# Attention probabilities turned in 32x32 blocks by VectorE, value products on row tiles of 32, heads in two groups

## The chip, the cores and the metric

The kernel runs on one core of one Trainium2 chip. The metric is the device time of one execution in microseconds (us), as the median of several runs. All inputs start in the chip's main memory and all outputs end there.

## The reference

One step of a decoder layer over two inputs at once: a prompt of 512 tokens, and one new token for each of eight running sequences ("samples"). The width is 1024, and everything is float32. Cut to what matters here:

```python
h = einsum('btd,de->bte', x, w_in)                  # 1024 -> 3600 columns
qa, ka, va, za, ga, qb, kb, vb, gb = split(h)       # mixer A: 4 heads; mixer B: 8 heads of 64
o_a, s_new = gla_chunked(...)                       # mixer A: gated linear attention, chunks of 64
# mixer B, prompt: every query reads earlier keys at three strides
for window, dil in ((128, 1), (512, 4), (2048, 16)):
    p = exp(logits + bias - m)                      # logits = q.k / 8
    outs.append(einsum('bhqj,bqjhd->bhqd', p, vg) / s)
o_b = merge of the three, weighted by their sums
mix = concat([o_a * silu(ga), o_b * silu(gb)])
y   = einsum('bte,ed->btd', mix, w_out)
x_new = layer_norm(alpha * x + y)
# outputs: x_new, the GLA states, and the new key and value rows
```

For the prompt the three strided patterns make one causal attention over 512 keys, in which a key's weight carries how many of the patterns reach it. So mixer B is, for each head: scores (512 x 512, the lower triangle in blocks of 128), an exponential with a bias table, a normalization by the row's sum, and the product of the probabilities with the values.

## The kernel before, in words

**Engines and order.** No order of instructions is written down. Each part of the work is a Python generator that yields operations and conditions; `add(gen, rank)` hands it to a planner (class `Plan`), which issues, at each step, the operation that its cost model lets start first, and among equals the one of the lowest rank. `T`, `V`, `S`, `G` and `D` are TensorE (PE in the profile), VectorE (DVE), ScalarE (ACT), GpSimd (POOL) and SyncE's DMA queue (SP). A `Batch` is issued without anything between; `At(name, n)` waits until a mark was set n times. When two operations stand as a pair, the planner takes the engine that is done first: so `copy` goes to VectorE or ScalarE. Constants of the model (`LATE`, `SWITCH`, `SPARE` and transfer rates) shift what it chooses, not what an operation does. All instructions are issued from one line of code, L366 before and L368 after, so the profile tells them apart by tile names.

**Buffers.** `SLOTS` gives the number of buffers of each kind in SBUF (raw weights `r`, split weights `w`, 4 KB tiles `g`, probabilities `pr`, turned probabilities `pt`, bias strips `st` and so on), and `BANKS` the eight PSUM banks: three for projections (`d`), three for scores (`s`), two more (`t`).

**Projections.** PE's main work. Each weight and each input is split into a high and a low part (`hi_`, `lo_`), and three products are summed for each of eight blocks of 128 inputs. `feature` makes columns on partitions (two halves of 256 tokens, the first with the eight samples beside it); `token` makes tokens on partitions. The order is ka, qa, qb, kb, vb, gb, va, ga, and then the output projection (`ps_y`, `ps_yf`). Weights come group by group over SP's queue (`weight_loads`, tiles `raw`).

**Mixer B of the prompt, the part that changes.** `strips` builds the bias strip of each head and query half, two buffers' worth ahead. `scores(m, pi, qt)` makes, for head pair m and query half pi, the score blocks of two query blocks in one batch of PE (tile `ps_s`). `softmax(h, q, ...)` then does, for one head and one query block of 128: a multiply with the strip and a row maximum on VectorE (shown as CUSTOM_DVE_ANT_0, `pr<-ps_s,strip`), an exponential on ScalarE, a reciprocal and a scale. The probabilities lie with queries on partitions; the product with the values needs keys there. So each 128x128 block goes through PE's transpose into `ps_pt`, and `copy` brings it to `pt`, one tile for each head and query half:

```python
for k in range(q + 1):
    yield T.transpose(pt[:, k * P:k * P + P], pr[:, k * P:k * P + P], ident)
yield copy(B[f"pt{h}{pi}"][:, :q + 1, qs], pt[:, :n]...)
```

There are 80 such blocks. `weighted(g, pi)` waits for the four heads of group g in query half pi, and issues one batch: for each key block and head, 64 columns of values as the weights (128 rows of contraction) and up to 256 queries as the moving side, into one bank `ps_pv`. One `copy` brings the bank to `obT`. There are four such batches. `mix_b` multiplies `obT` by the gate `gb` and splits the product for the output projection.

**Other work at the same time.** Mixer A's chunks on PE are short runs of small products (`ps_l`, `ps_og`, `ps_kv`, `ps_oa`). The samples' attention over the cached keys and values is elementwise work of GpSimd and VectorE (`past`, `vv`). `keys_store` brings the 512 key rows of the prompt to memory, as 16 transfers at the end of the kernel; `values_store` does the same for the values.

Of the kernel before, what the change touches and what calls it, by code (L numbers as in the profile page):

```python
# [62 lines left out]
    g=24,  # L63
    w=6, r=2,
    sv=5,
    pt=4,
    t2=3, st=3,
    pr=4,
    t1=6, ob=4,
# [6 lines left out]
LATE = 1600.0  # L76
SWITCH = 105
PIECE = 256
SPARE = 800.0


class Op:
# [3 lines left out]
    def __init__(self, eng, fn, args, kw):  # L86
# [13 lines left out]
        if fn == "dma_start":  # L100
# [4 lines left out]
            rate = 60 if run <= 128 else 175 if x.ap[0][1] <= 64 else 340 if run >= 4096 else 230  # L105
# [265 lines left out]
def trunk(ctx: ExitStack, tc: tile.TileContext, xT, xp, xs, state, ck, cv, w_in, wab, gnorm,  # L371
# [140 lines left out]
    order = [g for k, g in groups.items() if k not in ("ka0", "ka1")] + wo  # L512
# [33 lines left out]
    def first_loads():  # L546
# [16 lines left out]
        add(weight_loads(), 3)  # L563
# [9 lines left out]
    def first_splits():  # L573
# [27 lines left out]
        add(weight_splits(), 4)  # L601
# [83 lines left out]
    def gates(n, own):  # L685
        for u in range(2):
            yield from make(f"{n}{u}", Need("g", f"{n}{u}", [P, 4, 256]))
        for i in range(4):
            yield from feature(groups[f"{n}{i}"], gate_into(n, own, i))

    def dense():
# [24 lines left out]
        add(gate_decay(pz), 10)  # L716
# [5 lines left out]
        for i in range(2):  # L722
            yield from feature(groups[f"qa{i}"], into("qa", qa_s, i, 0.125))
        for x in ("qh0", "ql0", "qh1", "ql1"):
            yield from make(x, Need("g", x, [P, 4, 256], F32R), 4)
        for i in range(4):
            yield from feature(groups[f"qb{i}"], parts("q", q_s, i, 0.125))
        for i in range(4):
            yield from make(f"kp{i}", Need("g", f"kp{i}", [P, 2, 512], F32R), 2)
            yield from feature(groups[f"kb{i}"], parts("k", k_s, i, 1.0))  # L730
        for u in range(2):
            yield from make(f"v{u}", Need("g", f"v{u}", [P, 2, 512]))
        for i in range(2):
            yield from token(groups[f"vb{i}"], *vb_into(i))
        yield from gates("gb", gb_s)
        for u in range(2):
            yield from make(f"va{u}", Need("g", f"va{u}", [P, 2, 512]))
        for i in range(2):
            yield from token(groups[f"va{i}"], *va_into(i))
        yield from gates("ga", ga_s)  # L740
        free(*xt)
        for t in range(TT):
            add(residual(t), 8)
# [153 lines left out]
    def gla_state():  # L897
# [3 lines left out]
        yield At("qb", 8)  # L901
# [114 lines left out]
    def parts(n, own, m, scale):  # L1016

        def evac(ps, u):
            if n == "q":
                h, l = (B[f"q{x}{u}"][:, m, :] for x in "hl")  # L1020
            else:
                h, l = (B[f"kp{m}"][:, x, u * 256:u * 256 + 256] for x in range(2))
            yield S.mul(h, ps[:, :256], scale)
            yield V.scalar_tensor_tensor(l, ps[:, :256], scale, h.bitcast(F32), op0=ALU.mult, op1=ALU.subtract)
            if u == 0:
                yield S.mul(own[:, m, :], ps[:, 256:TW[0]], scale)
            mark(f"{n}b{m}{u}")
            mark(f"{n}b")
            if n == "k":
                add(keys_out(ps, m, u), 2)  # L1030
            else:
                free(ps)
        return evac

    def keys_out(ps, m, u):
# [6 lines left out]
        mark("kw")  # L1042

    def keys_store():

        yield At("kw", 8)
        yield At("y0_done", 1)
        for i in range(2):
            kw = B[f"kw{i}"].rearrange("p m (b j) -> p m b j", j=32)
            for m in range(2):  # L1050
                for a in range(4):
                    c = (2 * i + m) * P + a * 32
                    yield D.dma_start(kw_p[:, c:c + 32].rearrange("(b i) j -> i b j", i=32), kw[a * 32:a * 32 + 32, m])
            free(B[f"kw{i}"])
# [30 lines left out]
    def vb_into(i):  # L1085
        def evac_f(ps, f):
            c = slice(i * GW + f * P, i * GW + f * P + P)
# [4 lines left out]
            yield copy(B["v0"][:, :, c], ps[:, :GW].rearrange("p (t c) -> p t c", t=2))  # L1092
            free(ps)
            mark(f"vb{i}0")

        def evac(ps, t):
            yield copy(B["v1"][:, t - 2, i * GW:i * GW + GW], ps)
            free(ps)
            mark(f"vb{i}1")
        return evac_f, evac  # L1100

    def values_store(u):
        for i in range(2):
            yield At(f"vb{i}{u}", 2)
        yield D.dma_start(vw_p[u * GW:u * GW + GW, :].rearrange("(t p) c -> p t c", p=P), B[f"v{u}"])

    def strips():
        yield At("tab")
        yield At("qb", 1)
        for pi in range(2):  # L1110
            w = 256 * (pi + 1)
            for h in range(HB):
# [9 lines left out]
    def scores(m, pi, qt):  # L1122
# [8 lines left out]
        own = pi  # L1131
        for v in range(2):
# [8 lines left out]
        kp, qx = B[f"kp{m}"], [B[f"q{x}{pi}"] for x in "hl"]  # L1141
        yield Batch(T.matmul(ps[v, q][:, cols[q]], qx[a][v * 64:v * 64 + 64, m, (q % 2) * P:(q % 2) * P + P],
# [3 lines left out]
        for v in range(2):  # L1146
# [3 lines left out]
            for q in qt:  # L1150
                add(softmax(2 * m + v, q, ps[v, q], pr[v, q], cols[q]), 31 + 20 * pi / 100 + m / 50)

    def softmax(h, q, ps_all, pr_all, cols):
# [3 lines left out]
        qs = slice(j * P, j * P + P)  # L1157
# [10 lines left out]
        if j == 0:  # L1168
            yield from make(f"pt{h}{pi}", Need("pt", f"pt{h}{pi}", [P, 2 * pi + 2, 256]))
        else:  # L1170
            yield At(f"pt{h}{pi}")
# [6 lines left out]
        mark(f"p{h}{pi}")  # L1178
        if h == HB - 1 and j == 1:
            mark("scores")  # L1180

    def weighted(g, pi):
# [5 lines left out]
        for h in hs:  # L1188
            yield At(f"p{h}{pi}", 2)
        for u in range(pi + 1):  # L1190
            yield At(f"vb{g}{u}", 2)
        yield from make(f"obT{pi}{g}", Need("ob", f"obT{pi}{g}", [P, 2, 256]), 2)
        pv = yield bank(("s", "t"), f"ps_pv{g}{pi}")
        last = 2 * pi + 1
        pts = [B[f"pt{h}{pi}"] for h in hs]
        every = [(k, h) for k in range(last + 1) for h in range(4)]
# [3 lines left out]
        free(*pts)  # L1200
        yield copy(B[f"obT{pi}{g}"].rearrange("p m t -> p (m t)"), pv)
        free(pv)
        for m in (2 * g, 2 * g + 1):
            mark(f"ob{pi}{m}")
            mark(f"ob{pi}")
        if plan.marks[f"ob{pi}"] == 4 and pi:
            free(B["v0"], B["v1"])

    def sample_queries():
# [3 lines left out]
        for bi in range(NB):  # L1213
            qbc = yield Need("t2", f"qbc{bi}", [P, 512])
            yield D.dma_start(qbc, qsd[bi:bi + 1, :].to_broadcast([P, 512]))
            past = yield Need("sv", f"past{bi}", [P, 2, 512])
            yield D.dma_start(past, ck[bi])
            add(sample_logit(bi, past, qbc), 50)

    def sample_logit(bi, past, qbc):  # L1220
        for k in range(2):
            for c in range(0, 512, PIECE):
                x = past[:, k, c:c + PIECE]
                yield G.tensor_tensor(x, x, qbc[:, c:c + PIECE], op=ALU.mult)
        yield V.tensor_reduce(lt[:, :, bi * 8:bi * 8 + 8], past.rearrange("p k (h d) -> p k h d", d=64), axis=AX.X, op=ALU.add)
        free(past, qbc)
        mark("lt")

    def sample_softmax():
# [17 lines left out]
        raw = yield Need("pr", "cts_raw", [66, T_W - T_D])  # L1247
# [47 lines left out]
    def sample_value(bi, vv, pb):  # L1295
        vf = vv.rearrange("p k f -> p (k f)")
        pf = pb.rearrange("p m k -> p (m k)")
        for c in range(0, 2 * 512, PIECE):
            x = vf[:, c:c + PIECE]
            yield G.tensor_tensor(x, x, pf[:, c:c + PIECE], op=ALU.mult)  # L1300
        yield V.tensor_reduce(o_pv[:, :, bi], vf.rearrange("p (m k) -> p m k", m=4), axis=AX.X, op=ALU.add)
        free(vv, pb)
# [93 lines left out]
    def gate_into(n, own, m):  # L1396
        def evac(ps, u):
# [7 lines left out]
            yield V.tensor_tensor(B[f"{n}{u}"][:, m, :], ps[:, :256], sg[:, :256], op=ALU.mult)  # L1405
# [8 lines left out]
    def mix_tiles(n, u):  # L1414
# [3 lines left out]
        else:  # L1418
            yield At(f"ob{u}0")
            yield At(f"gb{u}0")  # L1420
        for x in "hl":
            yield from make(f"m{x}{n}{u}", Need("g", f"m{x}{n}{u}", [P, 4, TW[u]], F32R))
# [21 lines left out]

    def mix_b(u, m):
        yield At(f"ob{u}{m}")
        yield At(f"gb{u}{m}")
        yield At(f"mlb{u}")
        gb = B[f"gb{u}"][:, m, :]
        yield V.tensor_tensor(gb, gb, B[f"obT{u}{m // 2}"][:, m % 2], op=ALU.mult)  # L1450
        free(B[f"obT{u}{m // 2}"])
        yield from split(gb, B[f"mhb{u}"][:, m, :GW], B[f"mlb{u}"][:, m, :GW])
        mark(f"mix_b{u}{m}")
        mark(f"mix_b{u}")
        if plan.marks[f"mix_b{u}"] == 4:
            free(B[f"gb{u}"])
# [10 lines left out]
    def mix_sample_b():  # L1467
        yield At("gb_s", 4)
        yield At("o_bs")
        yield At("mlb0")  # L1470
        yield V.tensor_tensor(gb_s, gb_s, o_bs, op=ALU.mult)
        yield from split(gb_s, B["mhb0"][:, :, GW:], B["mlb0"][:, :, GW:])
# [21 lines left out]
    def out_unit(t, c, w):  # L1494
# [3 lines left out]
        for k in range(KT):  # L1498
            yield g.at(k)
            yield At(f"mix_b{u}{k}") if k < 4 else At(f"mix_a{u}", t % 2 + 1)  # L1500
            mh, ml = (B[f"m{x}{'ba'[k // 4]}{u}"][:, k % 4, tl] for x in "hl")
# [15 lines left out]
    def out_half(g, f, ps, ks):  # L1517
        w, c = wo[g // 2], g % 2 * GW + f * P
        for k in ks:
# [3 lines left out]
            mh, ml = (B[f"m{x}{'ba'[k // 4]}0"][:, k % 4, :] for x in "hl")  # L1523
# [98 lines left out]
    add(fills(), 9)  # L1622
    add(dense(), 100)
    add(bias_table(), 60)
# [132 lines left out]
```

## Time and profile before

| what | value |
|---|---|
| median of 3 runs | 283.76 us (283.2 to 284.01) |
| the profiled execution's own time | 283.35 us |
| its span, first to last instruction | 281.5 us |
| granted TensorE clock, mean | 0.991 |
| busy share of the span | PE 96%, weight loads 90%, VectorE 73%, ScalarE 56%, GpSimd 20% |
| DMA | 52.27 MB, mean 186 GB/s |

The profile is one execution. PE counts matmuls and PEld the weight loads that run beside them. A busy share is a mean over stages with different limits. The groups name an operation by its output and inputs (`out<-in`), with partitions x elements and a count; behind the bars stand busy time, the mean duration of one in ns, and the idle time before it with what ended it. In the chain of waits each row is a start, a duration and the work that was on the path at that time; "issue" is time in which the engine waited for nothing that the profile shows. PE's float32 products leave two records each; those on split inputs one.

### The profile page before, as it was taken

The page shows a single profiled execution, that of the slowest core. Times are in us where ns is not written, and L with a number is a line of the kernel's source. Part 1 is how long each engine was busy: PE and PEld are TensorE (multiplying, and loading weights), DVE is VectorE, ACT ScalarE, POOL GpSimd, SP SyncE. Part 2 cuts the span into 40 slices and gives each one's busy share as a digit, 9 for nine tenths or more (in the row PEclk, how much of TensorE's full clock was granted, in tenths as well). Part 3 has the DMA queues.
Part 4 walks back from the last instruction along what each step waited for, and adds up shares of the span by engine and source line. Part 5 has one row for each costly group of instructions (what it writes and reads, how often), then busy time and mean ns, then how long its engine had stood idle before and what let it go on. Part 6 is the DMA issues. An engine that isn't in the chain of part 4 may idle for free.

```text
span 281.5 us, 7063 instructions
## 1 busy us (share of the span) xinstructions
PE 271.2 (96%) x2760; PEld 253.3 (90%) x2760; DVE 206.2 (73%) x501; ACT 158.5 (56%) x448; POOL 55.4 (20%) x72
## 2 busy tenths in 40 slices
PE   8999999999999999999999999999999999999980
PEld 5899999999989999998979989999899999997880
DVE  3856799978967956649768885537987997539575
ACT  4748754514745974668677863425589955413011
POOL 4000000000282472700003535824500000000000
PEclk9999999999999999999999999999999999999996
DMA  7966628323876798647499889599563499865203
GB/s 201 286 173 187 184 77 220 83 77 108 276 219 180 236 285 241 160 160 230 155 226 179 231 225 265 119 251 191 180 198 102 150 336 255 189 139 197 105 2 149
DMA packets 59944, 52.27 MB, mean 186 GB/s; under 512 B 12506, under 2 KB 50692, under 8 KB 59910
## 3 DMA queue, kind: packets, MB, share of 16 engines
q1 hardware_dynamic: 59802, 51.73, 67.3%
q8 instruction: 22, 0.36, 0.6%
q14 instruction: 12, 0.10, 0.1%
q10 hardware_dynamic: 108, 0.07, 0.1%
HBM read 46.24 MB, written 6.03 MB: 186 GB/s over the span
## 4 chain that ended last, share of the span: by engine, by line
PE 91%; DVE 4%; DMA 2%; ACT 1%; issue 1%; SPq 0%; DVEq 0%
PE ps_ga L366 8%; PE ps_gb L366 8%; PE ps_qb L366 8%; PE ps_yf L366 8%; PE ps_y L366 7%; PE ps_kb L366 7%; PE ps_va_f L366 4%; PE ps_qa L366 4%; PE ps_vb_f L366 4%; PE ps_va L366 4%; PE ps_vb L366 4%; PE ps_pt L366 3%; PE ps_pv L366 3%; PE ps_s L366 3%; PE ps_ka L366 3%; DMA x_raw<-in_xT_dram 2%
## 5 line engine op out<-in xcount | busy, mean ns | idle before, releaser
L366 POOL TENSOR_TENSOR past<-past,qbc 128x256 f32<-128x256 f32 x32 | 25.3, 824 | 89.0 <-DMA past<-in_ck_dram 89.0
L366 POOL TENSOR_TENSOR vv<-vv,pb 128x256 f32<-128x256 f32 x32 | 26.9, 872 | 55.7 <-DMA pb<-psd_s 47.8
L366 ACT ACTIVATE pr<-pr,ms 128x128 f32<-128x128 f32 (+3 forms) x47 | 24.8, 545 | 5.9 <-DVE ms L366 5.9
L366 DVE CUSTOM_DVE_ANT_0 pr<-ps_s,strip 128x128 f32<-128x128 f32 (+3 forms) x32 | 14.5, 479 | 2.6 <-PE ps_s L366 2.5
L366 PE MATMUL ps_pt<-cf,pr 128*128 128x128 f32 x80 | 13.6, 275 | 0.3 <-DVE pr L366 0.3
L366 PE MATMUL ps_ka<-xx,hi_ka 128*128 128x264 f32 (+1 forms) x64 | 13.4, 306 | 0.5 <-DVE xx L366 0.5
L366 ACT ACTIVATE sg<-sg 128x264 f32<-128x264 f32 (+1 forms) x32 | 13.6, 426 | 0.3
L366 ACT COPY pt<-ps_pt 128x256 f32<-128x256 f32 (+3 forms) x25 | 10.4, 431 | 5.8 <-PE ps_pt L366 5.6
L366 PEld LDWEIGHTS ps_ka<-xx,hi_ka 128*128 128x128 f32 x64 | 10.9, 203 | 1.5 <-DVE xx L366 0.9
L366 ACT ACTIVATE d<-d 128x512 f32<-128x512 f32 x11 | 6.8, 643 | 6.7 <-DVE d L366 6.7
L366 PEld LDWEIGHTS ps_pt<-cf,pr 128*128 128x128 f32 x80 | 9.3, 140 | 1.1 <-issue 1.0
L366 ACT ACTIVATE rstd<-mv 128x1 f32<-128x1 f32 x4 | 0.7, 203 | 16.8 <-DVE mv L366 16.8
L366 DVE TENSOR_REDUCE o_pv<-vv 128x4 f32<-128x1024 f32 x8 | 9.7, 1210 | 0.2 <-POOL vv L366 0.2
L366 DVE TENSOR_REDUCE lt<-past 128x16 f32<-128x1024 f32 x8 | 9.6, 1204 | 0.0
L366 PE MATMUL ps_pv<-pt,v 128*64 128x256 f32 (+1 forms) x96 | 9.5, 348 | 0.0
L366 PE MATMUL ps_ka<-xx,lo_ka 128*128 128x264 f32 (+1 forms) x32 | 9.4, 293 | 0.0
L366 PEld LDWEIGHTS ps_pv<-pt,v 128*64 128x64 f32 x96 | 6.3, 137 | 2.9
L366 DVE TENSOR_SCALAR pr<-pr,ms 128x512 f32<-128x512 f32 (+3 forms) x17 | 8.4, 498 | 0.4
L366 ACT COPY feat_y<-ps_yf 128x256 f32<-128x256 f32 x8 | 3.0, 372 | 9.9 <-PE ps_yf L366 9.9
L366 DVE TENSOR_TENSOR xx<-x_raw,xx 128x520 fp32r<-128x520 f32 (+2 forms) x9 | 5.8, 640 | 3.6 <-ACT xx L366 3.5
L366 PE MATMUL ps_s<-kp,qh 64*128 64x128 f32 (+3 forms) x64 | 8.3, 344 | 0.0
L366 DVE TENSOR_TENSOR d<-b 128x1024 f32<-128x1024 f32 x6 | 7.3, 1217 | 0.0
(529 smaller groups left out, 1028.1 us busy)
## 6 DMA issues: line engine op xcount, KB each, us to landing
past<-in_ck_dram SPq DMA_DIRECT2D x8, 512.0 KB
vv<-in_cv_dram SPq DMA_DIRECT2D x8, 512.0 KB
pb<-psd_s SPq DMA_DIRECT2D x16, 256.0 KB
s<-in_state_dram SPq DMA_DIRECT2D x4, 512.0 KB
qbc<-qsd SPq DMA_DIRECT2D x8, 256.0 KB
strip<-tabr SPq DMA_DIRECT2D x8, 256.0 KB
y<-in_xp_dram SPq DMA_DIRECT2D x4, 512.0 KB
x_raw<-in_xT_dram SPq DMA_DIRECT2D x7, 260.0 KB
```

Source lines behind the costliest of these rows:

```text
L366: getattr(eng.eng, op.fn)(*op.args, **op.kw)
```

## The change

It does five things.

1. The probabilities are turned by one VectorE instruction for each head and query block, `V.transpose`, which transposes each 32x32 block in its place and leaves the blocks where they are. PE's 80 transposes and the 32 copies from PSUM are gone. `pt` is one tile for each head now, with all four query blocks.
2. After that, the four row blocks of 32 partitions in `pt` belong to the four 32-blocks of queries in each query block; the columns go by 32-blocks of keys, and within one the 32 keys lie on the partitions and the 32 queries on the columns. So a value product contracts over 32 rows only. For row block r, key block k and rotation d, `probs` picks the columns of the key 32-block (r + d) mod 4, in all query blocks from k on. The values of those keys must lie on the same 32 partitions: `values_rotate(g)` makes three copies of each value tile, rotated by 32, 64 and 96 partitions, by DMA within SBUF (tiles `vr`, two transfers each).
3. `weighted(g)` runs once for each group of four heads, with all 512 queries: 256 products of 32 rows and 64 columns (4 key blocks x 4 rotations x 4 heads x 4 row blocks), with 128, 96, 64 or 32 moving columns, into four banks, one for each row block of queries, and four copies to `obT`.
4. Tiles `qh`, `ql`, `gb`, `mhb`, `mlb` and the value tiles are cut by head group in place of token half. The scores of the second head group wait until the first group's value batch has its banks (`At("pv0")`). The value projection vb0 comes ahead of kb2.
5. Buffers, model constants and the ranks of nearly all tasks are set anew. The key rows are stored in two parts in the middle, and no longer at the end.

The diff, cut to its core:

```diff
-    g=24,
-    w=6, r=2,
+    g=21,
+    w=7, r=3,
...
-    t2=3, st=3,
+    t2=2, st=2,
...
-    t1=6, ob=4,
+    t1=5, ob=2,
...
-LATE = 1600.0
-SWITCH = 105
+LATE = 1300.0
+SWITCH = 140
...
-SPARE = 800.0
+SPARE = 1100.0
+
+ORDER = "qa0 qa1 qb0 qb1 qb2 qb3 kb0 kb1 vb0 kb2 kb3 vb1 gb0 gb1 gb2 gb3 va0 va1 ga0 ga1 ga2 ga3".split()
...
-            rate = 60 if run <= 128 else 175 if x.ap[0][1] <= 64 else 340 if run >= 4096 else 230
+            rate = 130 if run <= 128 else 175 if x.ap[0][1] <= 64 else 340 if run >= 4096 else 230
...
-        yield At("kw", 8)
-        yield At("y0_done", 1)
...
+        yield At(f"kw_in{i}", 4)
...
+    def values_rotate(g):
...
+        yield At(f"vb{g}", 4)
+        vr = yield Pair(*(Need("g", f"vr{g}{d}", [P, TT, GW]) for d in range(1, 4)))
+        for d, r in enumerate(vr, 1):
+            B["vr", g, d] = r
+            c = P - d * 32
+            yield D.dma_start(r[:c], B[f"v{g}"][d * 32:])
+            yield D.dma_start(r[c:], B[f"v{g}"][:d * 32])
+            mark(f"vr{g}")
...
+        if m > 1:
+            yield At("pv0")
...
-        if j == 0:
-            yield from make(f"pt{h}{pi}", Need("pt", f"pt{h}{pi}", [P, 2 * pi + 2, 256]))
+        if q == 0:
+            yield from make(f"pt{h}", Need("pt", f"pt{h}", [P, 3 * 384 + NP]))
...
-        pt = yield bank("t", f"ps_pt{h}{q}")
-        for k in range(q + 1):
-            yield T.transpose(pt[:, k * P:k * P + P], pr[:, k * P:k * P + P], ident)
+        yield V.transpose(B[f"pt{h}"][:, q * 384:q * 384 + n], pr)
         free(pr_all)
-        yield copy(B[f"pt{h}{pi}"][:, :q + 1, qs], pt[:, :n].rearrange("p (k t) -> p k t", t=P))
-        free(pt)
...
         hs = range(4 * g, 4 * g + 4)
         for h in hs:
-            yield At(f"p{h}{pi}", 2)
...
+            yield At(f"p{h}", TT)
+        yield At(f"vr{g}", 3)
+        yield from make(f"obT{g}", Need("ob", f"obT{g}", [P, 2, NP]), 4)
+        pv = yield Pair(*(bank(("s", "t"), f"ps_pv{g}{r}") for r in range(4)))
+        mark(f"pv{g}")
...
-        yield Batch(T.matmul(pv[h % 2 * 64:h % 2 * 64 + 64, h // 2 * GW + (P if k == last else 0):h // 2 * GW + GW],
-                             B[f"v{k // 2}"][:, k % 2, (4 * g + h) * 64:(4 * g + h) * 64 + 64], pts[h][:, k, P if k == last else 0:],
-                             start=k == 0 and h < 2, stop=k == last, skip_group_check=True) for k, h in every)
...
+        def probs(h, r, k, d):
+            x = pts[h][r * 32:r * 32 + 32]
+            return bass.AP(tensor=x.tensor, offset=x.offset + k * 384 + k * P + (r + d) % 4 * 32, ap=[x.ap[0], [384, TT - k], [1, 32]])
+
+        yield Batch(T.matmul(pv[r][h % 2 * 64:h % 2 * 64 + 64, h // 2 * P + k * 32:h // 2 * P + P],
+                             vs[d][r * 32:r * 32 + 32, k, h * 64:h * 64 + 64], probs(h, r, k, d),
+                             start=k + d == 0 and h < 2, stop=k + d == 6, skip_group_check=True)
+                    for k in range(TT) for d in range(4) for h in range(4) for r in range(4))
+        free(*pts, *vs)
+        ob = B[f"obT{g}"].rearrange("p m (q r t) -> p m q r t", r=4, t=32)
+        for r in range(4):
+            yield copy(ob[:, :, :, r, :], pv[r][:, :2 * P].rearrange("p (m q t) -> p m q t", m=2, t=32))
+            free(pv[r])
```

More of the change, by code (lines that the diff above doesn't have):

```diff
@@ L511, in trunk @@
     wo = [Group(w_out, g * 512, f"wo{g}_", 512) for g in range(2)]
-    order = [g for k, g in groups.items() if k not in ("ka0", "ka1")] + wo
+    order = [groups[k] for k in ORDER] + wo
     def weight_loads():
@@ L683, in into, with project @@
         return evac
[L685 to L689, printed above, removed]
+    def project(n, i):
+        g = groups[f"{n}{i}"]
+        if n == "qa":
+            yield from feature(g, into("qa", qa_s, i, 0.125))
+        elif n == "qb":
+            if i % 2 == 0:
+                for x in "hl":
+                    yield from make(f"q{x}{i // 2}", Need("g", f"q{x}{i // 2}", [P, 2, NP], F32R), 4)
+            yield from feature(g, parts("q", q_s, i, 0.125))
+        elif n == "kb":
+            yield from make(f"kp{i}", Need("g", f"kp{i}", [P, 2, 512], F32R), 2)
+            yield from feature(g, parts("k", k_s, i, 1.0))
+        elif n == "vb":
+            yield from make(f"v{i}", Need("g", f"v{i}", [P, TT, GW]), 2)
+            yield from token(g, *vb_into(i))
+        elif n == "va":
+            if i == 0:
+                for u in range(2):
+                    yield from make(f"va{u}", Need("g", f"va{u}", [P, 2, 512]))
+            yield from token(g, *va_into(i))
+        elif n == "gb":
+            if i % 2 == 0:
+                yield from make(f"gb{i // 2}", Need("g", f"gb{i // 2}", [P, 2, NP]))
+            yield from feature(g, gate_into("gb", gb_s, i))
+        else:
+            if i == 0:
+                for u in range(2):
+                    yield from make(f"ga{u}", Need("g", f"ga{u}", [P, 4, 256]))
+            yield from feature(g, gate_into("ga", ga_s, i))
     def dense():
@@ L721, in dense @@
                 add(into("ka", ka_s, i, 1.0)(pk[i, u], u), 2)
[L722 to L740, printed above, removed]
+        for name in ORDER:
+            yield from project(name[:2], int(name[2]))
         free(*xt)
         for t in range(TT):
-            add(residual(t), 8)
+            add(residual(t), 46.7)
         add(residual_sample(), 8)
@@ L1109, in strips @@
         yield At("qb", 1)
-        for pi in range(2):
+        for h0, pi in ((0, 0), (0, 1), (4, 0), (4, 1)):
             w = 256 * (pi + 1)
-            for h in range(HB):
+            for h in range(h0, h0 + 4):
                 yield At(f"kb{h // 2}{pi}")
@@ L1175, in softmax, with weighted @@
         free(pr_all)
-        yield copy(B[f"pt{h}{pi}"][:, :q + 1, qs], pt[:, :n].rearrange("p (k t) -> p k t", t=P))
-        free(pt)
[L1178 to L1182, printed above, removed]
+        mark(f"p{h}")
+    def weighted(g):
         hs = range(4 * g, 4 * g + 4)
         for h in hs:
-            yield At(f"p{h}{pi}", 2)
[L1190 to L1196, printed above, removed]
-        yield Batch(T.matmul(pv[h % 2 * 64:h % 2 * 64 + 64, h // 2 * GW + (P if k == last else 0):h // 2 * GW + GW],
-                             B[f"v{k // 2}"][:, k % 2, (4 * g + h) * 64:(4 * g + h) * 64 + 64], pts[h][:, k, P if k == last else 0:],
-                             start=k == 0 and h < 2, stop=k == last, skip_group_check=True) for k, h in every)
-        free(*pts)
-        yield copy(B[f"obT{pi}{g}"].rearrange("p m t -> p (m t)"), pv)
-        free(pv)
@@ L1203, in weighted @@
         for m in (2 * g, 2 * g + 1):
[L1204 to L1207, printed above, removed]
+            for u in range(2):
+                mark(f"ob{u}{m}")
+                mark(f"ob{u}")
     def sample_queries():
@@ L1443, in mix_a, with mix_of @@
             free(ga)
+    def mix_of(n, u, k):
+        if n == "a":
+            return [B[f"m{x}a{u}"][:, k, :] for x in "hl"]
+        return [B[f"m{x}b{k // 2}"][:, k % 2, TS[u]] for x in "hl"]
     def mix_b(u, m):
+        g = m // 2
         yield At(f"ob{u}{m}")
         yield At(f"gb{u}{m}")
[L1448 to L1452, printed above, removed]
+        yield At(f"mlb{g}")
+        gb = B[f"gb{g}"][:, m % 2, u * GW:u * GW + GW]
+        yield V.tensor_tensor(gb, gb, B[f"obT{g}"][:, m % 2, u * GW:u * GW + GW], op=ALU.mult)
+        free(B[f"obT{g}"])
+        yield from split(gb, *(x[:, :GW] for x in mix_of("b", u, m)))
         mark(f"mix_b{u}{m}")
-        mark(f"mix_b{u}")
-        if plan.marks[f"mix_b{u}"] == 4:
-            free(B[f"gb{u}"])
+        mark(f"mixed{g}")
+        if plan.marks[f"mixed{g}"] == 4:
+            free(B[f"gb{g}"])
     def mix_sample_a():
@@ L1470, in mix_sample_b @@
         yield At("mlb0")
+        yield At("mlb1")
         yield V.tensor_tensor(gb_s, gb_s, o_bs, op=ALU.mult)
-        yield from split(gb_s, B["mhb0"][:, :, GW:], B["mlb0"][:, :, GW:])
+        for g in range(2):
+            yield from split(gb_s[:, 2 * g:2 * g + 2], *(B[f"m{x}b{g}"][:, :, GW:TW[0]] for x in "hl"))
         mark("mix_sb")
```

127 lines of the change are left out of this document (64 added, 63 removed).

## The prediction

> **What bounds the kernel now.** I read the page's shares first, then PE's waits, the chain of waits in order of time, the stages as windows, and the instruction queue.
>
> ```profile
> PE 271.2 (96%) x2760; PEld 253.3 (90%) x2760; DVE 206.2 (73%) x501; ACT 158.5 (56%) x448; POOL 55.4 (20%) x72
> ...
> PE 91%; DVE 4%; DMA 2%; ACT 1%; issue 1%; SPq 0%; DVEq 0%
> ...
> q8 instruction: 22, 0.36, 0.6%
> ...
> PE warm_ps L366 <- DVE warm L1617: 1.2, 1, 1.2
> PE ps_ka L366 <- DVE xx L366: 0.5, 2, 0.3
> PE ps_qb L366 <- issue: 0.5, 1, 0.5
> PE ps_pt L366 <- DVE pr L366: 0.3, 1, 0.3
> ```
>
> PE is busy for 96% of the span and makes 91% of the chain. The last four rows are everything that PE waited for. So a microsecond taken from PE comes off the time, and one added to PE or made PE wait goes onto it. The other engines count only where they make PE wait. PE's rows of the stages that the change touches, from the chain of waits (start, us, what, records):
>
> ```profile
> 46.52 2.00 PE ps_l L366 x128
> ...
> 54.48 1.01 PE ps_og L366 x32
> 55.49 2.00 PE ps_l L366 x128
> 57.49 0.44 PE ps_qb L366 x2
> 57.94 0.50 issue
> ...
> 106.27 1.45 PE ps_pv L366 x16
> ...
> 122.95 1.45 PE ps_pv L366 x16
> ...
> 142.18 3.18 PE ps_pv L366 x32
> ...
> 157.03 0.76 PE ps_pt L366 x7
> ...
> 166.01 3.18 PE ps_pv L366 x32
> ...
> 193.56 1.03 PE ps_kv L366 x32
> ...
> 212.13 2.12 PE ps_oa L366 x96
> ```
>
> **Removed: the transposes of the probabilities on PE.** Seven transposes in a row take 0.76 us, 0.109 us each.
>
> ```profile
> L366 PE MATMUL ps_pt<-cf,pr 128*128 128x128 f32 x80 | 13.6, 275 | 0.3 <-DVE pr L366 0.3
> ```
>
> The group's mean of 275 ns overlaps with its neighbours, so I take the chain's pace: 80 x 0.109 = 8.7 us off PE. The four old batches of value products cost 1.45 + 1.45 + 3.18 + 3.18 = 9.3 us and go as well.
>
> **Added: two batches of 256 value products.** Each product has 32 rows of contraction and 64 columns of weights, so eight lie on PE side by side: four row tiles by two column tiles. In the old batches every f32 product left two records (48 products, 96 records), so a batch now has 512 records, in rounds of eight, 16 rounds at each moving width of 128, 96, 64 and 32. Do eight really run at once? ps_oa's 96 records are 32 on four tiles and 64 on eight. At ps_kv's pace (four tiles, 32 records in 1.03 us) the 32 take 1.03, which leaves 1.09 us for the 64; on four tiles they would need 2.06. So yes, on two row groups by four column groups; four by two is not in the trace. Price of a round: width 256 and 128 together give the old batches' 3.18 us for 12 rounds of 256 and 4 of 128 on two tiles, so 0.227 us for 256 and 0.114 for 128. Width 96 is three quarters of that, 0.086. For 64 and 32 a floor holds: ps_l loads 64 columns for a width of 32 and needs 2.00 us for 32 rounds, 0.0625 each. A batch is 16 x (0.114 + 0.086 + 0.0625 + 0.0625) = 5.2 us, both 10.4. On work alone PE loses 8.7 and gains 1.1.
>
> **Whether the instructions come in time** decides the sign. PE has 2760 matmuls and as many weight loads, 5520 instructions, and the instruction queue brought 22 packets with 0.36 MB: one packet feeds 251 instructions. At the usual pace of a projection that lasts over 14 us:
>
> ```profile
> 22.90 10.27 PE ps_qa L366 x84
> ```
>
> (10.27 / 84 is 0.122 us for a load and a matmul.) ps_og and ps_l, back to back, are 160 records, so 320 instructions in 3.01 us; two records later PE stops for 0.50 us with nothing that the profile can name. A single ps_l, 256 instructions (at 46.52), has no such stop behind it. My reading: PE holds the packet it executes and the next one, and a run longer than that waits for a packet. From 54.48 to 58.44 it executed 324 instructions in 3.95 us: 251 in 3.1 us. A new batch has 1024 instructions, 4.1 packets, and needs one each 1.3 us. With the first at hand and three awaited, it takes 3 x 3.1 + 1.3 = 10.6 us instead of 5.2, both 21.2. The ends: the queue's share of 0.6% of 16 engines' 281.5 us is 27 us, 1.23 us a packet, which would cost nothing (10.4); a packet for each 3.95 us gives 3 x 3.95 + 1.3 = 13.2, both 26.4. I take 3.1, the only stretch in which PE ran dry.
>
> The Trainium skill, "Runtime: NRT & Kernel Launch", section Instruction fetch mechanics, says that the sequencer streams 16 KiB blocks of 256 instructions by itself while the current one executes, at a cost "mostly hidden"; by it the batches stay at 5.2 us, the first rival below. The trace agrees with the block's size and disagrees at the one row of 0.50 us.
>
> In the new order of PE's instructions ps_og no longer stands next to a ps_l (31 projection matmuls stand before ps_og and 19 behind it): the 0.50 us go.
>
> **Moved to other engines.** VectorE turns 32 blocks of 128 to 512 columns.
>
> ```profile
> L366 DVE STREAM_TRANSPOSE kw<-ps_kb 128x256 f32<-128x256 f32 x8 | 3.5, 443 | 1.1 <-ACT k_s L366 1.1
> ...
> L366 DVE CUSTOM_DVE_ANT_0 pr<-ps_s,strip 128x512 f32<-128x512 f32 x8 | 5.4, 680 | 0.1
> ...
> L366 DVE CUSTOM_DVE_ANT_0 pr<-ps_s,strip 128x128 f32<-128x128 f32 x8 | 2.2, 275 | 0.0
> ...
> L366 DVE COPY pt<-ps_pt x7: 281/558/692, 108.0 to 157.4; 128x384 f32<-128x384 f32 x3, 128x128 f32<-128x128 f32 x2, 128x256 f32<-128x256 f32 x1, 128x512 f32<-128x512 f32 x1
> ```
>
> 443 ns at 256 columns, and 0.135 us for each 128 more or less as in the other two rows ((680 - 275) / 3): 0.31, 0.44, 0.58 and 0.71, eight of each, 16.3 us. About 3.4 us of VectorE's copies of transposes go (seven, near 0.5 each). That is +12.9 us on VectorE in the stretch of the scores:
>
> ```profile
> 64.00:95.00 31.00, 30.66 (x369) 29.62 (x362) 26.26 (x66) 17.77 (x55) 12.97 (x16) 1.00 0.65 198
> 95.00:127.00 32.00, 32.00 (x279) 29.94 (x278) 20.17 (x59) 21.05 (x61) 12.35 (x16) 1.00 0.75 218
> 127.00:165.00 38.00, 38.00 (x319) 34.60 (x317) 31.33 (x86) 30.26 (x75) 9.38 (x12) 1.00 0.83 208
> ```
>
> (PE, loads, VectorE, ScalarE, GpSimd; then clock, DMA share, GB/s.) VectorE goes from 77.8 to 90.7 us. With starved batches PE's side of this stretch is 101 - 8.7 + 11.9 = 104 us, so VectorE is 87% full, as in 64 to 95 now (26.26 of 31): I cost it at nothing, and PE's own waits are what hides it. ScalarE loses 25 copies and gains eight smaller ones: nothing.
>
> Six rotated copies of the values, 0.5 MB each, join SP's queue and the DMA engines: 3 MB at some 210 GB/s are 14 us of DMA, spread over some 60 us whose share is 0.75 to 0.83. In the new order each set stands behind key stores and ahead of the va weights. The keys' 16 stores come from the end to the middle:
>
> ```profile
> 236.15 14.01 SPq L366 DMA_DIRECT2D out_dram<-kw  x16
> ```
>
> 0.88 us of SP each. What hides them is one more raw weight buffer (three for two) and one more split one (seven for six); if that cover goes, a late weight group stops PE for what is missing, 1 to 3 us. Whole heads now wait in one batch for 16 softmaxes, and behind it on PE stand the gb and va projections. From the last scores to each batch PE has 84 and 96 projection matmuls, 10 and 11.7 us, against about 9 and 10.6 us of VectorE work in its order: nothing, or 1 to 2 us if it lags. The last normalization is the same.
>
> **The sum**, against the profiled execution's own 283.35 us: - 8.7 (transposes) - 9.3 (old products) + 21.2 (new ones) - 0.5 (the old stop) = 286.1. The median of the runs is 0.4 above the profiled one: 286.4. Its own bounds, from packets every 2.5 us to every 3.95 us: 283 to 292.
>
> **Rivals.** *Packets are in time.* For it: 22 packets came and one stop of 0.50 us is all that shows; one case is thin. Against it: a stop exactly behind the longest fast run. Then 283.35 - 8.7 - 9.3 + 10.4 - 0.5 = 275.3, plus up to 3 us of VectorE's lag as PE no longer waits: 277 with the 0.4. It decides if a packet takes under 1.3 us. Faster, chance 0.25.
>
> *VectorE becomes the bound.* With packets in time the stretch of 101 us would have to shrink to 93, and VectorE's 90.7 us would fill 97% of it. No stretch above shows more than 85%; at 90% the stretch takes 101 us again and the gain is gone: 283, between 281 and 286. For it: two thirds of the added work stand in chains score, exponential, scale, turn. Against it: PE's 24 to 96 matmuls of cover. 0.12.
>
> *Records, not columns, price a product.* If ps_l's 2.00 / 128 = 0.0156 us were a floor for every record, 1024 records take 16.0 us: 280.9, 281.3 with the 0.4. Against it: ps_oa's 1.09 us for 64 records is 0.017, explained as well by width. 0.05. The Trainium skill, "TensorE: Matmul & The Clock Gate", section "Wait — 56ns, not 53.3ns?", gives a floor of about 25 ns from start to start; by it the batches take 25.6 us and the kernel 290.5. ps_l's 15.6 ns speaks against that floor here, so it gets no chance of its own.
>
> **How the numbers follow.** Forecast 0.58. A change of 0.3%, 0.85 us, is about what a measurement of this kernel can tell from none. Faster: 0.25 + 0.05 + 0.04 of VectorE + 0.03 of the forecast's low end = 0.37; within: 0.07 + 0.03 = 0.10; slower: 0.48 + 0.05 = 0.53. The range 276.8 to 290 leaves out the fastest part of the first rival (about 0.1) and packets slower than some 3.6 us (0.08). Alone, the forecast would have 283 to 290.
>
> **What would show it.** Right: two batches ps_pv near 10 us each in the chain, with stops put down to issue inside them and some 28 packets on the instruction queue (5520 - 160 - 192 + 2048 = 7216 instructions). Batches near 5 us without such stops make it the first rival; near 8 us with even pace, the third. PE waiting for VectorE's pt ahead of ps_pv, or for ps_s's banks, is the second. Rows "PE <- DMA raw" would mean that SP's queue was late. ps_pt must be gone. It is wrong if PE's idle time hardly grows.

## The result, and the profile after

The changed kernel takes 305.33 us (304.87 to 307.1, four runs), against 283.48 us for the kernel before in the same comparison: 1.077 times as long, 95% interval 1.074 to 1.081. Here and below a median is of all executions, while a ratio and its interval leave out the executions in a slower state, at a lower clock or over 1.5% above the fastest of their kernel. The profiled execution took 307.1 us with a span of 305.3. From the page of the kernel after, the busy shares, the chain and the instruction queue, and then what PE waited for most:

```profile
PE 275.6 (90%) x3608; PEld 259.3 (85%) x3608; DVE 214.3 (70%) x520; ACT 149.6 (49%) x435; POOL 54.3 (18%) x72
...
PE 74%; DVE 9%; issue 7%; ACT 6%; DMA 3%; SPq 0%; DVEq 0%
...
q8 instruction: 28, 0.46, 0.6%
...
PE ps_pv L368 <- issue: 17.8, 6, 5.2
PE warm_ps L368 <- DVE warm L1651: 1.2, 1, 1.2
PE ps_gb L368 <- DVE gb L368: 1.1, 1, 1.1
```

PE's idle time grew from 10.3 to 29.7 us (span less busy time), and nearly all of the growth is one row: six stops inside ps_pv, 17.8 us, with nothing behind them that the profile names. VectorE has a smaller share of the longer span than before (70% for 73%). The two value batches in the chain of waits (start, us, what):

```profile
123.97 3.37 PE ps_pv L368 x191
127.34 2.12 issue
129.46 1.66 PE ps_pv L368 x81
131.12 4.26 issue
135.38 1.82 PE ps_pv L368 x104
137.20 1.63 issue
138.83 0.64 PE ps_pv L368 x21
...
180.55 2.81 PE ps_pv L368 x172
183.36 5.15 issue
188.51 2.62 PE ps_pv L368 x114
191.14 3.02 issue
194.16 2.15 PE ps_pv L368 x105
196.31 1.58 issue
197.89 1.17 PE ps_pv L368 x58
199.06 3.92 PE ps_va L368 x17
```

The first batch lasts from 123.97 to 139.47, 15.5 us, the second from 180.55 to 199.06, 18.5 us. (The chain drops some records of a run; in the trace the middle runs are 128 records long, 256 instructions with their weight loads, one packet.) The last row shows a second loss: 17 projection matmuls take 3.92 us, 0.23 us each, where the prediction's row for ps_qa had 0.122. The windows around the batches say why (PE, loads, VectorE, ScalarE, GpSimd; then clock, DMA share, GB/s):

```profile
124.00:136.00 12.00, 5.62 (x425) 5.33 (x427) 3.25 (x16) 4.29 (x14) 2.87 (x4) 1.00 0.72 211
136.00:139.50 3.50, 1.87 (x113) 1.69 (x101) 0.76 (x3) 0.09 (x1) 0.00 (x0) 0.52 0.57 167
139.50:146.40 6.90, 6.90 (x36) 6.45 (x37) 1.61 (x3) 2.05 (x5) 0.00 (x0) 0.50 0.58 148
146.40:180.40 34.00, 32.42 (x262) 30.71 (x261) 30.78 (x89) 23.08 (x67) 6.58 (x8) 1.00 0.84 179
...
187.30:199.00 11.70, 5.88 (x321) 5.49 (x320) 0.00 (x0) 0.00 (x0) 5.76 (x9) 0.50 0.23 68
199.00:204.40 5.40, 5.40 (x29) 5.40 (x26) 2.14 (x5) 3.90 (x9) 0.00 (x0) 0.50 0.00 0
```

Around the stops of 4.26 and 5.15 us the granted clock falls to 0.50, and it stays there while PE works again: 6.9 us behind the first batch and 5.4 us behind the second. At half speed these 12.3 us do the work of 6.1.

So the account of the profiled execution: 283.35 - 8.7 (transposes) - 9.3 (old products) - 0.5 (the old stop) + 34.0 (both batches) + 6.1 (half clock behind them) = 305.0. Other waits of PE grew from 0.8 to 3.2 us (all its rows of waits, without the first one of 1.2 and without issue), which gives 307.4 against 307.1 measured.

### The profile page after: what moved, and what is told of

It is laid out like the page before. It is cut to its first block, busy times and chain, and to the rows that moved or that the text cites. A ratio compares the mean times of both kernels' runs of the same rounds, so it can differ in the third digit from the quotient of the medians.

```text
span 305.3 us, 8766 instructions
## 1 busy us (share of the span) xinstructions
PE 275.6 (90%) x3608; PEld 259.3 (85%) x3608; DVE 214.3 (70%) x520; ACT 149.6 (49%) x435; POOL 54.3 (18%) x72
## 4 chain that ended last, share of the span: by engine, by line
PE 74%; DVE 9%; issue 7%; ACT 6%; DMA 3%; SPq 0%; DVEq 0%
PE ps_qb L368 8%; PE ps_kb L368 8%; PE ps_yf L368 8%; PE ps_y L368 7%; PE ps_pv L368 5%; PE ps_ga L368 5%; PE ps_va L368 4%; PE ps_gb L368 4%; PE ps_qa L368 4%; PE ps_vb_f L368 4%; PE ps_va_f L368 3%; DMA raw_ka<-in_w_in_dram 3%; PE ps_s L368 3%; DVE pr L368 2%; PE ps_l L368 2%
## 5 line engine op out<-in xcount | busy, mean ns | idle before, releaser
L368 POOL TENSOR_TENSOR vv<-vv,pb 128x256 f32<-128x256 f32 x32 | 25.7, 834 | 81.3 <-DMA pb<-psd_s 81.3
L368 PE MATMUL ps_pv<-pt,vr 32*64 32x128 f32 (+3 forms) x768 | 15.0, 282 | 17.8 <-issue 17.8
L368 ACT ACTIVATE pr<-pr,ms 128x128 f32<-128x128 f32 (+3 forms) x50 | 26.2, 542 | 8.8 <-DVE ms L368 8.4
L368 PEld LDWEIGHTS ps_pv<-pt,vr 32*64 32x64 f32 x768 | 12.8, 163 | 18.7 <-issue 18.7
L368 DVE STREAM_TRANSPOSE pt<-pr 128x128 f32<-128x128 f32 (+3 forms) x32 | 15.0, 491 | 10.1 <-PE ps_pv L368 9.4
L368 ACT COPY obT<-ps_pv 128x256 f32<-128x256 f32 x8 | 2.4, 387 | 29.2 <-PE ps_pv L368 29.2
L368 DVE TENSOR_TENSOR gb<-gb,obT 128x256 f32<-128x256 f32 x8 | 3.1, 416 | 18.8 <-ACT obT L368 18.8
L368 DVE COPY_PREDICATED near<-cm,ps_l 128x256 f32<-128x256 uint8 x12 | 6.3, 545 | 3.9 <-PE ps_l L368 3.7
L368 PE MATMUL ps_gb<-xx,hi_gb__1666 128*128 128x264 f32 (+1 forms) x32 | 8.3, 360 | 0.5 <-ACT v L368 0.5
L368 ACT COPY feat_y<-ps_yf 128x256 f32<-128x256 f32 x8 | 3.0, 370 | 10.2 <-PE ps_yf L368 10.2
```

What stands on the lines that cost most here:

```text
L368: getattr(eng.eng, op.fn)(*op.args, **op.kw)
```

## Experiments

Theories, as the expectations number them. 1: PE gets packets of 256 instructions too slowly for a batch that executes one in 1.5 us. 2: the regrouping and the ranks cost the time. 3: the 32-row tiles themselves stop PE. 4, 5 and 6 come up below, for what is left when the stops are gone. In the tables, "packets" is PE's waits put down to issue, "others" its other waits without the first one of 1.2 us, both summed from the rows of PE's waits in the profiled execution.

**The stops made in the kernel before.** No part of the change is in this kernel, only more instructions in a row:

```diff
-                    for i, (_, _, ks, qs) in enumerate(made)
+                    for _ in range(4) for i, (_, _, ks, qs) in enumerate(made)
```

> The kernel before, with the products of mixer A's levels (ps_l) made four times over into the same places (same outputs): batches of 512, 512 and 256 records, 1024, 1024 and 512 instructions, on 64-row tiles, with no change elsewhere. By their own pace of 2.00 us for 128 records they add 15 us. Theory 1, a packet of 256 instructions each 3.7 us at best: the large batches take 12 to 14 us in place of 8.0, with stops put down to issue after runs of 128 records and a granted clock below 1 behind them; 283.4 + 15 + 2 x 5 + some 3 to 6 for the clock = 311 to 315 us. Theory 3, stops belong to 32-row tiles or to the rotated copies: no stops, 298.5 us.

Measured: 323.45 us (one execution), and all three batches have 512 records, not two of 512 and one of 256. Their own added work is thus 3 x 6.0 = 18 us. From its chain of waits, two of the three batches, and the window of the first of these:

```profile
68.57 4.02 PE ps_l L366 x265
72.58 0.82 issue
73.40 2.06 PE ps_l L366 x128
75.47 1.66 issue
77.13 3.15 PE ps_l L366 x119
...
88.43 3.27 PE ps_l L366 x214
91.71 1.57 issue
93.28 2.61 PE ps_l L366 x128
95.89 1.12 issue
97.01 3.64 PE ps_l L366 x128
100.73 1.49 PE ps_l L366 x42
...
62.00:82.00 20.00, 17.52 (x591) 16.70 (x584) 7.36 (x14) 4.35 (x9) 0.00 (x0) 0.84 0.01 3
```

After some 210 to 265 records comes the first stop, then runs of exactly 128 records. From the start of one such run to the start of what follows it are 3.73 us each time (73.40 to 77.13, 93.28 to 97.01, 97.01 to 100.73; in the last of these the clock is 0.50, and PE's own work fills 3.64 of it). In the window shown the DMA engines are at 1% and 3 GB/s. So neither the 32-row tiles (these are 64 rows) nor other transfers are needed for the stops: 256 instructions took 3.73 us here once PE lived from packet to packet, 14.6 ns an instruction. The clock of 0.84 shows the half clock again. Theory 1's time of 311 to 315 was for one batch less: with three large ones its sum is 283.4 + 18 + 3 x 5 + 4.5 to 9 for the clock = 321 to 325. Theory 3 fails.

**A quarter of the instructions.** The same columns pass through PE; a product takes all 128 rows:

```diff
-                             vs[d][r * 32:r * 32 + 32, k, h * 64:h * 64 + 64], probs(h, r, k, d),
+                             vs[d][:, k, h * 64:h * 64 + 64], probs(h, k, d),
...
-                    for k in range(TT) for d in range(4) for h in range(4) for r in range(4))
+                    for k in range(TT) for d in range(4) for h in range(4))
```

> The changed kernel, with each value batch made of 64 products over all 128 rows in place of 256 products over 32 (each rotation goes to one bank; what is left out is the sorting of the queries by row block, so the attention output of the prompt is another one). The columns that pass through PE in a round, VectorE's turns, the rotated copies and all waits stay; PE's instructions for a batch fall from 1024 to 256, one packet. Theory 1, PE runs out of instruction packets: no stop put down to issue in ps_pv, a batch near 5.2 us, the granted clock stays at 1.00 behind it, and the time is 305.3 - 17.8 (stops) - about 6 (batches' own work, 16 to 10.4) - about 6 (projections at half clock) = 275 us. Theory 2, the new grouping, ranks and waits cost the time, and the stops are only where it shows: over 295 us.

Measured: 288.78 us (one execution; the same kernel with one t2 buffer more, below, took 288.02 to 290.11 in four). From its chain of waits, and what PE waited for:

```profile
170.52 5.05 PE ps_pv L368 x128
...
PE ps_yf L368 <- ACT oa L368: 3.9, 1, 3.9
PE ps_gb L368 <- DVE gb L368: 3.5, 2, 2.4
```

No stop, and a batch of 5.05 us. The stops, the batches' extra work and most of the half clock were worth 16.5 us of the 22. But 275 had been expected: some 14 us are missing, with PE waiting for ScalarE and VectorE at places where it hadn't waited before: 11.1 us without the first 1.2, where the kernel before had 0.8. The clock, expected at 1.00, was 0.50 for 10.2 us in and behind the two longest of these waits, worth up to 5 us. Waits and clock together account for the missing time.

**The same instructions, spread.** Four pieces of 64 products with projection steps between them:

```diff
+        for i, ks in enumerate(((0,), (1,), (2,), (3,))):
+            if i:
+                yield At("steps", plan.marks["steps"] + 6)
...
-                    for k in range(TT) for d in range(4) for h in range(4) for r in range(4))
+                        for k in ks for d in range(4) for h in range(4) for r in range(4))
```

> The changed kernel, with each value batch cut into four pieces of 64 products (256 instructions, one packet), and at least six steps of a projection (18 matmuls, 2.2 us) ahead of each further piece. Same instructions and outputs. Theory 1, packets come late when PE executes one in under 3.7 us: the stops fall from 17.8 us to under 4, the clock stays near 1.00, and the time is 305.3 - 14 - 6 - 2 = about 281 to 285 us. Theory 2, grouping, ranks and waits: no gain from spreading, 300 us or more. Theory 3, it is the 32-row tiles themselves that stop PE: each piece holds a stop as before, 303 to 308 us.

> As the run before in this list, with five steps (15 matmuls, 1.8 us) in both batches. Same outputs. Theory 1: a piece and what lies behind it last 1.8 + 1.8 us, just under a packet's 3.7: stops under 6 us in all; 283 to 295 us. Theory 6: 300 us or more.

> The changed kernel with each value batch in four pieces of 64 products, at least four projection steps (12 matmuls, 1.5 us) apart in the first batch and ten (30 matmuls, 3.7 us) in the second. Same outputs. With six steps the stops had gone from 17.8 to 3.7 us, but PE then waited 10 us elsewhere and the time stayed at 304.8. Theory 1 with a wait of that one order of engines: the second batch has no stop (a packet in more than 5 us), the first one some; 283 to 295 us. Theory 6, whatever PE wins at the batches it gives back in waits for other engines, since these work up to the time at which the slow batches ended: 300 us or more again.

> As the runs before in this list, with four steps (12 matmuls, 1.5 us) in both batches. Same outputs. Theory 1: a piece and what lies behind it last 1.8 + 1.5 us, under a packet's 3.7: some stops, under 8 us in all; 285 to 297 us. Theory 6: 300 us or more.

| steps between pieces | against before, 95% interval | packets, us | others, us | mean clock |
|---|---|---|---|---|
| none (the changed kernel) | 1.077 (1.074 to 1.081) | 17.8 | 3.2 | 0.947 |
| 6 | 1.078 (1.072 to 1.083) | 3.7 | 15.1 | 0.961 |
| 5 | 1.052 (1.046 to 1.057) | 9.0 | 5.9 | 0.979 |
| 4, and 10 in the second batch | 1.064 (1.058 to 1.070) | 7.5 | 13.4 | 0.972 |

With four steps in both batches the time is 1.056 (1.051 to 1.061) times that of before; its profile is of an execution of 437.67 us at a clock of 0.56, and gives no row for the table. Spreading does to the stops what theory 1 says, in the main: 17.8 us become 3.7 to 9.0, with the same tiles and the same number of instructions, so theory 3 is out here as well. Two of its figures were missed: with five steps under 6 us were expected, and with ten steps in the second batch none there, where 3.4 and 2.7 remain. The time follows only in part: in none of the four runs did it come down to theory 1's range (304.8 us for 281 to 285, 298.3 and 302.4 for 283 to 295, and, by its ratio, about 299 for 285 to 297). With six steps one wait takes nearly all of it back; its rows of PE's waits:

```profile
PE ps_yf L368 <- ACT mhb L368: 10.0, 1, 10.0
PE ps_va_f L368 <- issue: 3.0, 1, 3.0
```

The planner writes one order for all engines, and each edit gives another one; in this order the output projection stands 10 us ahead of the last split of the mix on ScalarE. With five steps there is no such wait, and packets, clock and time go together: 298.3 us, 7 less. So theory 6 describes two of these orders, not a law.

**The regrouping alone.** Turning by PE, value products over 128 rows, no rotated copies, all else as changed:

```diff
-        yield V.transpose(B[f"pt{h}"][:, q * 384:q * 384 + n], pr)
+        for k in range(q + 1):
+            yield T.transpose(pt[:, k * P:k * P + P], pr[:, k * P:k * P + P], ident)
+        yield copy(B[f"pt{h}"][:, q * 384:q * 384 + n], pt[:, :n])
```

> The changed kernel with the turning on PE again (80 transposes and copies from PSUM) and value products over 128 rows (two batches of 16 products, no rotated copies); head groups, order of projections, buffers (one t2 buffer more) and ranks as in the changed kernel. Same outputs. Theory 1: PE has the old work, no stops, clock 1.00: 283 us, up to 3 more for waits of the grouping. Theory 2, grouping, ranks and waits cost the time: 295 us or more.

Measured: 288.42 us, 1.015 (1.011 to 1.020); no stops, clock 0.993, other waits of 5.6 us in place of 0.8. Theory 2 fails for the bulk of the 22 us, but some 4 to 5 us belong to the new grouping, buffers and ranks. To part these:

> The kernel with the turning on PE again and the new head groups and ranks (288.4 us), now also with the old order of the projections, the old constants of the planner's model, and no wait of the second group's scores for the first group's banks. Same outputs. If the order of projections and the wait cost the 5 us: 283 to 284.5 us. If the grouping by heads, the buffers and the ranks cost them: 287 us or more.

Measured: 1.020 (1.015 to 1.025), 289.02 us. Going back to the old order of the projections and the old constants, without the wait for pv0, did not bring the time back, so these are not the cause. The planner makes another order here too, so which of grouping, buffers and ranks it is stays open.

**What takes the gain when the stops are gone.** The kernel with a quarter of the instructions has 8 us less on PE than the regrouped one (two batches of 5.05 us for 8.7 + 9.3) and takes the same time. Two suspects: VectorE's 15 us of turning (theory 4) and the transfers of the rotated copies (theory 5).

> The changed kernel with 64 products over all 128 rows in each value batch (as in the run with a quarter of the instructions, whose attention output is another one), and one t2 buffer more. It is what the next two runs are compared with. The run with the quarter of the instructions had no stop for packets and was still 5 us above the kernel before, with some 8 us less work on PE; PE waited for ScalarE and VectorE instead. Theory 4: with the stops gone VectorE and ScalarE set the pace. Theory 5: the transfers do (rotated copies, key rows, strips, on one queue). Both: 285 to 290 us here.

> As the run with 128 rows and one t2 buffer more, and the turning left out as well: the scale writes the probabilities straight into pt, so VectorE has 32 instructions and 15.0 us less (the attention output is another one). Theory 4, VectorE's added 15 us are what PE waits for: under 281 us, at best 276. Theory 5, the transfers: within 2 us of its counterpart.

> As the run with 128 rows (two t2 buffers), and the twelve transfers that make the rotated copies of the values left out, 3 MB, as are their six tiles (the products read the plain values; the attention output is another one). Theory 5, transfers: 3 to 6 us faster than the run with 128 rows, 283 to 286 us. Theory 4, VectorE: within 2 us of 288.8.

| value products over 128 rows, and | against before, 95% interval | others, us | mean clock |
|---|---|---|---|
| one t2 buffer more | 1.021 (1.017 to 1.025) | 9.7 | 0.971 |
| that, and no turning | 1.026 (1.022 to 1.030) | 10.6 | 0.963 |
| no rotated copies (two t2 buffers) | 0.991 (0.988 to 0.994) | 7.2 | 0.982 |

Leaving out the 15 us of turning gives nothing, so theory 4 falls for these orders; VectorE's busy time fell by 9.5 us only (216.2 to 206.7), as the planner gave it other work. Without the copies the time falls by some 3%, about 8 us (288.8 to 0.991 x 283.4 = 280.8), which speaks for theory 5. The size is rough: the ten executions of that kernel lie between 279.1 and 288.1 us, with a median of 283.75, and its row of the table is from one of 283.96. How the copies hurt can be read on SP's queue in the kernel with a quarter of the instructions:

```profile
126.51 1.34 SPq L368 DMA_DIRECT2D strip<-tabr  x2
127.94 6.27 SPq L368 DMA_DIRECT2D vr<-v  x6
135.38 0.38 SPq L368 DMA_DIRECT2D raw_va__2160<-in_w_in_dram  x1
136.57 2.73 SPq L368 DMA_DIRECT2D strip<-tabr  x2
```

The next two strips, for which the scores of the second group wait, go out 10 us after the ones before them. But without the copies they went out no earlier (136.07 us), so this place alone doesn't account for 8 us, and six tiles are free as well there. VectorE's waits for strips are 8.2 us with the copies and 0.8 without; but with one t2 buffer more they are 1.7 us, with the copies and at the same time of 289, so they don't settle it either. The last run was to decide:

```diff
+            for _ in range(2):
+                yield D.dma_start(r[:c], B[f"v{g}"][d * 32:])
+                yield D.dma_start(r[c:], B[f"v{g}"][:d * 32])
```

> The run with 128 rows (288.8 us; its attention output is another one) with each of the rotated copies of the values made twice over: twelve transfers and 3 MB more on the same queue at the same places. Leaving them out had given 280.7 us. If the transfers themselves cost those 8 us (queue and bandwidth), doubling them costs 5 to 8 us: 294 to 297 us. If it was the freed buffers or another order of the engines: within 2 us of 288.8.

Measured: 318.4 us, 1.121 (1.114 to 1.128), which neither side had expected. Its rows of PE's waits show why it doesn't decide:

```profile
PE ps_pv L368 <- DMA vr<-v: 25.7, 3, 14.5
```

The second writing of a tile went to a late place in SP's queue, and the batches, already begun, waited for it. That copies which land late are costly is shown; what their bandwidth costs is not. Whether the 8 us are the transfers, the six freed tiles or another order stays open.

## Why the prediction was wrong

The direction and the mechanism held: PE ran out of instruction packets in the two batches, 28 packets came as worked out, ps_pt was gone, and the kernel is slower. The size was off: +21.9 us where +2.6 was forecast, above the range's end of 290.

- **The term "3 x 3.1 + 1.3 = 10.6 us" for a batch is the step that failed.** Measured: 15.5 and 18.5, 12.8 us more for both. The 3.1 us a packet came from a stretch of 324 instructions that crossed one stop, so its mean counted instructions that were there already. Runs from packet to packet take 3.73 us with nearly idle DMA engines, and 3.45 to 5.92 in the changed kernel (129.46, 135.38, 138.83 and 188.51, 194.16, 197.89). The upper bound of 3.95 us a packet, from the same stretch, was no upper bound either.
- **All packets were priced alike, and some came late.** With 3.73 the same formula gives 12.5 a batch, 25.0 for both: 3.8 of the 12.8 us. Part of the rest shows in the trace's records of the instruction packets. A packet's own transfer takes 0.9 to 1.3 us in these batches. It starts 1.0 to 1.5 us after the run before it has begun where the DMA engines are at 30% or less (135.38 to 136.48, at 5%), but 3.3 and 3.0 us after it in the two longest periods (129.46 to 132.78, at 88%; 188.51 to 191.54, at 66%), and only at 186.02 in the stop of 5.15 us that begins at 183.36, with the engines full. The late packets thus stand where other transfers were on their way. That these held them up is not shown by a run that varies them alone.
- **The half clock was not in the sum.** 6.1 us behind the batches, and part of the 18.5 within the second. The profile before had no stop long enough to show it, but the Trainium skill has the rule: "TensorE: Matmul & The Clock Gate", section HAM oscillation — how this bites in real kernels, says that an idle stretch of PE of over about 3.4 us throttles it to half speed, and that the penalty is half of the throttled time. The runs agree here: clock 0.50 from 136.13 and from 187.33 us, behind and in stops of 4.26 and 5.15. In the kernel with longer level batches no stop of 3.4 us was needed: its clock was 1.00 from 63.85 to 77.51 us and 0.50 from then to 84.33, with no stops before the fall but two of 0.82 and 1.66 us. A forecast that starves PE should have added this term.
- **The work of the batches**, 5.2 us each by rounds, was near: 6.1 us by the shortest runs of 128 records at each width in the kernels with pieces (1.83, 1.59, 1.38 and 1.27 us from first to last start). Eight products do run at once on four by two tiles: a round of eight at width 128 took 115 ns, as long as two products over 128 rows (55 ns each).
- **VectorE's turning at nothing** was right as far as the runs show: no wait of PE for VectorE's pt appears in the rows, and leaving the turning out brought no time in the kernel with products over 128 rows. Its size too: 15.0 us measured, 16.3 forecast.
- **The rest "at nothing"** was not quite: other waits of PE grew by 2.4 us here. With the stops taken away, 4 to 5 us show for grouping, buffers and ranks, and up to 8 that go away with the rotated copies. The first rival's 277 us was not reached even with packets in time: 288.8.
- **The Trainium skill's rule on fetching** ("Runtime: NRT & Kernel Launch", section Instruction fetch mechanics: the cost of a block boundary is "mostly hidden") holds for projections, which take over 14 us for a packet, and not for runs of small products. The measured 3.73 us a block decides.

## What to carry to other kernels

Count PE's instructions against time, weight loads included. In the batches here the first stop came after 192 to 265 records (384 to 530 instructions), in the kernel before after 162. Behind it 256 instructions cost 3.45 to 5.92 us whatever they computed, so a change that cuts products into small tiles pays by the number of instructions. Where PE starves, add the half clock behind the stops. And where one written order drives all engines, a microsecond won on PE is only won if the orders of the others still fit, so read PE's waits again after each edit, not the busy shares.

## What the runs showed of the hardware

- PE executes a packet of 256 instructions in as little as 1.3 us (128 records at width 32), but the next one started 3.45 to 3.73 us after it where the DMA engines were at 30% or less as it began, and 5.65 and 5.92 us after it where they were at 66% and 88%.
- On 32-row tiles a round of eight records took from 115 ns at width 128 (128 records in 1.83 us, sixteen rounds) to some 80 at width 32: 10 to 14 ns a record from start to start. The Trainium skill, "TensorE: Matmul & The Clock Gate", section "Wait — 56ns, not 53.3ns?", has the floor of about 25 ns that the prediction quoted; on these tiles it doesn't hold.
- Products over 128 rows with 64 columns of weights took, by the starts in the trace, 55, 40, 28 and 28 ns a record at the widths 128, 96, 64 and 32: below 64 columns a narrower product was no cheaper.
